# A decoder layer on one core: the sums for the up projection get a pool of their own, and the down projection's first tiles are staged in its room

## The chip, the cores and the metric

The kernel runs on one core of one Trainium2 chip. The core has a matrix engine (PE; its weight loads are listed apart as PEld), a vector engine (DVE), a scalar engine (ACT), GpSimd (POOL) and a sync engine (SP), which run side by side and wait for each other on semaphores. Transfers between DRAM and the on-chip memory (SBUF) are issued from an engine's queue (here almost all from SP's, some from POOL's) and land some microseconds later. The metric is the device time in microseconds (us); less is better. Before the change it is 2153.9 us, the median of three runs (2151.9 to 2154.32).

## The reference

One layer with 512 tokens of width 2048: token mixing, then a gated feed-forward block of width 5632 with a short causal convolution on one branch.

```
def conv_ffn(h, w_ffn_in, conv_w, conv_b, w_ffn_out):
    S = h.shape[1]
    up = h @ w_ffn_in
    a, b = up[..., :D_FF], up[..., D_FF:]
    a_pad = jnp.pad(a, ((0, 0), (CONV_W - 1, 0), (0, 0)))
    a = (conv_w[0] * a_pad[:, 0:S] + conv_w[1] * a_pad[:, 1:S + 1]
         + conv_w[2] * a_pad[:, 2:S + 2] + conv_b)
    return (jax.nn.gelu(a, approximate=True) * b) @ w_ffn_out
...
        h = rmsnorm(x, attn_pre_norm[l])
        m = token_mixer(h, w_in[l], ...)
        x = x + rmsnorm(m, attn_post_norm[l])
        h = rmsnorm(x, ffn_pre_norm[l])
        f = conv_ffn(h, w_ffn_in[l], conv_w[l], conv_b[l], w_ffn_out[l])
        x = x + rmsnorm(f, ffn_post_norm[l])
```

## The kernel before

**Numbers in two parts.** Every float32 operand of a large product is split into a high and a low part: ACT writes the high part (`whi` of a weight, L120; `ah` of an activation, L133), DVE the low part, operand minus high part (`wlo`, L121; `al`, L134). A product is then three matmuls: high by high, low by high, high by low. A "granule" is one weight tile of 128 x 1024 numbers (512 KB): its load, its `whi`, its `wlo`, and the matmuls that read them.

**Seven products for eight.** The up products (`h @ w_ffn_in`) and the down products (`@ w_ffn_out`) go by Winograd's form of Strassen's scheme: 2 x 2 blocks of activations and of weights, seven products of sums of blocks. A `Unit` runs seven segments, x0, z0, y0, z1, x1, y1, y2, which read the activation operands a11, s5, s2, s3, a12, s7, a22 in that order (s5, s2, s3, s7 are sums and differences of the a's), each with two granules. The weight sums are made on the way: POOL issues a DMA that adds a second weight block to a tile in place (`more`, L856), and DVE adds others (L872 in y0, L890 after y1). There are 20 up units (ten groups of 512 columns, two branches), then 10 down units (five chunks `c` of two groups, two halves `cb` of the output's columns). An up segment has 48 matmuls of 256 columns, a down segment 24 of 512. At the end `last_group` does the first 512 columns of the feed-forward width without the scheme, adds the shared part `accp` to the accumulators `acc` (L1128), and `finish` writes the output.

**From up to down.** After the last branch of a group, `token_sums` writes the group's blocks (a11, a12, a22) and, with DVE adds into tiles `s` (L975), its sums s5, s2, s7, s3 to DRAM (`sd0a`, `sd0s` for chunk 0, ... `sd4a`, `sd4s` for chunk 4). A tile `s` is one of two with tag "sum". `prepare(c, n)` (L993 to L996) loads operand n of chunk c from DRAM, 512 KB, and splits it into its place in `ah` and `al`. For chunk 0 it loads a11, s5, s2, s3 into free activation tiles (`flat_tile()`, rows named `u`), a12, s7, a22 later into staging tiles (`st`).

**Room in SBUF.** The up operands s5, s2, s3 (three sums in two parts, 6 tiles of 8 KB per partition), the tiles `s` and the p1 tiles lie in the pool `fa` up to the close:

```
    fa.close()
    sp3 = ctx.enter_context(tc.tile_pool(name="sp3", bufs=2, reuse_waits="tile"))
    ff = ctx.enter_context(tc.tile_pool(name="ff", bufs=2, reuse_waits="tile"))
    acc = [ff.tile([P, D], F32, name=f"acc{t}", bufs=1) for t in range(NT)]
```

`ff` holds the staging tiles (four with tag "st"), `acc`, `accp` and the gains `g3`; `sp3` holds spare granule tiles. They take `fa`'s room, so whoever writes there first waits for the last reader of what lay there.

**What sets the order.** The up and down units are ordered by a scheduler over the written program; each engine and SP's queue then run their own list in order. `to_ffn` (the norm ahead of the feed-forward block) and the last part of `last_group` are in hand-written order. In `to_ffn` the third token tile's `residual` (L647), `square` (L652) and `scale` (L658) stand among the loads and splits of weights (`weights_f`, L120 and L121) for matmuls at L156 to L158.

## Time and profile before

| | |
|---|---|
| device time, median of 3 runs | 2153.9 us (2151.9 to 2154.32) |
| profiled execution, its own time | 2150.73 us |
| its span | 2149.0 us |
| mean granted clock of PE | 0.995 |
| PE busy | 2110.2 us, 98% of the span |
| PEld busy | 1878.9 us, 87% |
| DVE busy | 1415.0 us, 66% |
| ACT busy | 899.1 us, 42% |
| POOL busy | 206.7 us, 10% |

The table is of one profiled execution; its span runs from its first to its last instruction. A row of the timeline has the start and the length in us, the engine, the line, the operation with output and input tiles, and in brackets how long the engine idled before it and what ended that. A row of the windows has a stretch, its length, the busy time and count of instructions of PE, PEld, DVE, ACT and POOL, then the granted clock of PE (1.00 is full), the DMA engines' share and GB/s. SPq and POOLq are the queues in which these engines issue transfers.

### The profile page before, as it was taken

To read this page: it belongs to the slowest core of one execution; us is meant where nothing else is said; L and a number is where in the kernel's file an instruction comes from. 1 tells how busy PE (TensorE), PEld (TensorE's weight loads), DVE (VectorE), ACT (ScalarE), POOL (GpSimd) and SP (SyncE) were. 2 spreads that over 40 slices of the span, in tenths; PEclk is the share of its full clock that TensorE was granted. 3 is DMA by queue.
4 is the path that set the end of the run, shared out by engine and by line. 5 is a ranking of instruction groups with operands and counts; after the bars stand their busy time and mean duration, and the time that the engine had idled before them with its cause. 6 is when DMAs were issued, how large, how long until landed. Compare 5 with 4: busy or idle time off the path is not lost.

```text
span 2149.0 us, 31874 instructions
## 1 busy us (share of the span) xinstructions
PE 2110.2 (98%) x13009; PEld 1878.9 (87%) x13009; DVE 1415.0 (66%) x1721; ACT 899.1 (42%) x1162; POOL 206.7 (10%) x245
## 2 busy tenths in 40 slices
PE   7999999999999999999999999999999899999997
PEld 6878888788888888999999999999999778888886
DVE  5345554443444237588777786787878777988987
ACT  4233332333343224344544553554454354544443
POOL 1000000000000000010111101111111011111101
PEclk9999999999999999999999999999999999999999
DMA  6322222222224234456775767667577677676663
GB/s 214 101 74 79 79 70 79 79 79 87 80 79 170 95 128 174 130 117 144 167 182 137 170 156 181 158 143 188 141 172 181 188 204 204 183 196 176 165 168 137
DMA packets 218470, 303.82 MB, mean 141 GB/s; under 512 B 11776, under 2 KB 155572, under 8 KB 216404
## 3 DMA queue, kind: packets, MB, share of 16 engines
q1 hardware_dynamic: 165204, 238.87, 33.0%
q0 software_dynamic: 53120, 62.92, 18.9%
q8 instruction: 102, 1.67, 0.3%
q14 instruction: 44, 0.36, 0.1%
HBM read 273.97 MB, written 27.79 MB: 140 GB/s over the span
## 4 chain that ended last, share of the span: by engine, by line
PE 39%; issue 16%; DVE 3%; DMA 2%; POOL 1%; ACT 1%; POOLq 0%; DVEq 0%; ACTq 0%
PE bank L908 7%; PE bank L909 7%; PE bank L907 7%; PE bank L1004 5%; PE bank L1005 4%; PE bank L1006 4%; PE bank L158 1%; PE bank L156 1%; PE bank L157 1%; DMA raw<-in_w_ffn_in_dram 1%; DVE wlo L121 1%; POOL rt L856 1%; DMA rt<-in_w_ffn_out_dram 1%; POOL raw L856 1%; DVE acc L1144 0%
## 5 line engine op out<-in xcount | busy, mean ns | idle before, releaser
L121 DVE TENSOR_TENSOR wlo<-raw,whi 128x1024 fp32r<-128x1024 f32 x332 | 404.1, 1221 | 371.5 <-ACT whi L120 354.5
L120 ACT ACTIVATE whi<-raw 128x1024 fp32r<-128x1024 f32 x332 | 350.9, 1060 | 647.5 <-PE bank L175 159.4
L120 ACT ACTIVATE whi<-rt 128x1024 fp32r<-128x1024 f32 x240 | 252.9, 1059 | 261.0 <-PE bank L908 157.4
L909 PE MATMUL bank<-ah,wlo 128*128 128x256 f32 x1280 | 353.6, 276 | 0.2 <-DVE wlo L121 0.2
L908 PE MATMUL bank<-al,whi 128*128 128x256 f32 x1280 | 353.4, 276 | 0.0
L907 PE MATMUL bank<-ah,whi 128*128 128x256 f32 x1280 | 353.3, 276 | 0.0
L121 DVE TENSOR_TENSOR wlo<-rt,whi 128x1024 fp32r<-128x1024 f32 x240 | 292.6, 1221 | 88.3 <-ACT whi L120 88.2
L174 PE MATMUL bank<-whi,ah 128*128 128x512 f32 x640 | 253.0, 398 | 0.4 <-ACT ah L133 0.4
L175 PE MATMUL bank<-wlo,ah 128*128 128x512 f32 x640 | 251.6, 394 | 0.1
L176 PE MATMUL bank<-whi,al 128*128 128x512 f32 x640 | 250.8, 394 | 0.0
L909 PEld LDWEIGHTS bank<-ah,wlo 128*128 128x128 f32 x1280 | 240.3, 188 | 0.4 <-DVE wlo L121 0.4
L908 PEld LDWEIGHTS bank<-al,whi 128*128 128x128 f32 x1280 | 240.3, 188 | 0.1
L907 PEld LDWEIGHTS bank<-ah,whi 128*128 128x128 f32 x1280 | 240.3, 188 | 0.1
L1005 PE MATMUL bank<-wlo,ah 128*128 128x512 f32 x560 | 219.9, 393 | 4.1 <-DVE wlo L121 4.1
L1004 PE MATMUL bank<-whi,ah 128*128 128x512 f32 x560 | 215.1, 393 | 6.6 <-ACT whi L120 4.7
L1006 PE MATMUL bank<-whi,al 128*128 128x512 f32 x560 | 219.1, 391 | 0.0
L156 PE MATMUL bank<-ah,whi 128*128 128x512 f32 (+1 forms) x576 | 215.1, 373 | 1.9 <-ACT whi L120 1.9
L158 PE MATMUL bank<-ah,wlo 128*128 128x512 f32 (+1 forms) x576 | 212.9, 370 | 0.8 <-DVE wlo L121 0.8
L157 PE MATMUL bank<-al,whi 128*128 128x512 f32 (+1 forms) x576 | 213.3, 370 | 0.0
L176 PEld LDWEIGHTS bank<-whi,al 128*128 128x128 f32 x640 | 120.8, 189 | 26.0 <-DVE al L134 0.3
L175 PEld LDWEIGHTS bank<-wlo,ah 128*128 128x128 f32 x640 | 121.0, 189 | 25.8 <-DVE wlo L121 1.0
L174 PEld LDWEIGHTS bank<-whi,ah 128*128 128x128 f32 x640 | 120.8, 189 | 24.9 <-ACT ah L133 0.8
(222 smaller groups left out, 3685.5 us busy)
## 6 DMA issues: line engine op xcount, KB each, us to landing
raw<-in_w_in_dram SPq DMA_DIRECT2D x96, 512.0 KB, 3.7
raw<-in_w_ffn_in_dram SPq DMA_DIRECT2D x96, 512.0 KB, 5.0
raw<-in_w_ffn_out_dram SPq DMA_DIRECT2D x48, 512.0 KB, 6.3
rt<-in_w_ffn_in_dram SPq DMA_DIRECT2D x40, 512.0 KB, 6.4
rt<-in_w_ffn_in_dram POOLq DMA_DIRECT2D x40, 512.0 KB, 5.9
raw<-in_w_ffn_in_dram POOLq DMA_DIRECT2D x40, 512.0 KB, 6.7
raw<-in_w_o_dram SPq DMA_DIRECT2D x32, 512.0 KB, 3.5
rt<-in_w_ffn_out_dram SPq DMA_DIRECT2D x20, 512.0 KB, 6.3
```

The lines of the kernel that those rows point to most:

```text
L120: act(hi, raw, AF.Copy)
L121: tt(lo, raw, hi.bitcast(F32), ALU.subtract)
L156: mm(o, wh, ah[:, t0:t1, kk, :], start=st, stop=False)
L174: mm(banks[t], ah[:, t, s, :], w[0][:, k, :], start=st, stop=False)
L175: mm(banks[t], ah[:, t, s, :], w[1][:, k, :], start=False, stop=False)
L176: mm(banks[t], al[:, t, s, :], w[0][:, k, :], start=False, stop=sp)
L907: mm(o, wh, sh[:, :, kk, :], start=start and kk == 0 and n == 0, stop=False, **NOW)
L908: mm(o, wh, sl[:, :, kk, :], start=False, stop=False, **NOW)
L909: mm(o, wl, sh[:, :, kk, :], start=False, stop=kk == HK - 1, **NOW)
L1004: mm(b[j], sh[:, o:o + P], w[0][:, q, :], start=start and st == 0, stop=False, **NOW)
L1005: mm(b[j], sh[:, o:o + P], w[1][:, q, :], start=False, stop=False, **NOW)
L1006: mm(b[j], sl[:, o:o + P], w[0][:, q, :], start=False, stop=st == 3, **NOW)
```

## The change

Six things are changed.

- The tiles of s5, s2, s3 of the up units move from pool `fa` to a pool `so`, which is closed after the last up unit's z1, the last segment that reads one of them (s3). Pool `ff` is opened there, in that room, with the four staging tiles, the spare granule tiles, `accp` and half of `acc`. Pool `fa` stays open to the end. The other half of `acc` and `g3` become activation tiles (`flat_tile()`), `acc` and `g3` go by halves of 1024 columns, and the small sums `ssf` go to another pool.
- `prepare` is parted: `stage(c, n)` loads into a staging tile, and `prepare` splits it. For chunk 0, a11, s5, s2, s3 are staged right after that z1, and a12, s7, a22 each as a staging tile comes free. The load of the first down unit's b22 weights has a name of its own (`fetch`) and is called ahead of the last up segment.
- In the last group's `token_sums`, s7 and s3 take the tag "p1" in place of "sum", so that its four sums have four tiles.
- The load of `g3` moves behind the first down unit, in two halves.
- In `to_ffn`, the weights' load and split `weights_f(wa, 0, 3, sp2)` stands ahead of `residual(3)`, where it stood behind `square(3)`.
- In `last_group` the adds of `accp` go by 512 columns (twelve of 128 x 512 for six of 128 x 1024), and the scratch tile of `gain` comes from `fa`. The padding behind `ident` is 32 numbers shorter.

```diff
--- before.py
+++ after.py
...
@@ -695,10 +695,10 @@
         ba = [bank(psm) for _ in range(2)]
         bb = [bank(psm) for _ in range(2)]
         mm_t(ba, 0, wa[0], 0, 2)
+        weights_f(wa, 0, 3, sp2)
         residual(3)
         turn(2, 0, 1, 2, 3)
         square(3)
-        weights_f(wa, 0, 3, sp2)
         mm_t(ba, 1, wa[1], 0, 2)
         mm_t(ba, 2, wa[2], 0, 2)
         scale(3)
@@ -734,8 +734,9 @@
 
     NG = NF // 4
     rp = ctx.enter_context(tc.tile_pool(name="rp", bufs=4, reuse_waits="tile"))
-    fa = ExitStack()
-    fp = fa.enter_context(tc.tile_pool(name="fa", bufs=2, reuse_waits="tile"))
+    fp = ctx.enter_context(tc.tile_pool(name="fa", bufs=2, reuse_waits="tile"))
+    sums = ExitStack()
+    so = sums.enter_context(tc.tile_pool(name="so", bufs=1, reuse_waits="tile"))
 
     ud0 = dram.tile([P, 4, S], F32, name="ud0")
     SN = ("a11", "a12", "a22", "s5", "s2", "s7", "s3")
@@ -786,7 +787,7 @@
     for n, (i, j) in part.items():
         up[n] = tuple(v[:, 2 * i:2 * i + 2, HK * j:HK * (j + 1), :] for v in (ah, al))
     for n in ("s5", "s2", "s3"):
-        up[n] = tuple(fp.tile([P, 2, HK, P], F32R, name=f"{n}{v}", bufs=1) for v in "hl")
+        up[n] = tuple(so.tile([P, 2, HK, P], F32R, name=f"{n}{v}", bufs=1) for v in "hl")
     s7raw = []
 
     def up_sums():
@@ -839,7 +840,7 @@
         def __init__(self, a, block, prods, chain, out):
             self.narrow = prods is up_prods
             self.a, self.block, self.prods, self.chain, self.out = a, block, prods, chain, out
-            self.banks = {}
+            self.banks, self.b22 = {}, None
 
         def run(self, seg, op, raws):
             c = seg[0]
@@ -866,8 +867,12 @@
             self.run("z0", "s5", self.t)
             self.out("z0", self.banks["z"])
 
+        def fetch(self):
+            self.b22 = [load(self.block(1, 1, g), self.a) for g in range(2)]
+
         def y0(self):
-            self.b22 = [load(self.block(1, 1, g), self.a) for g in range(2)]
+            if self.b22 is None:
+                self.fetch()
             for g in range(2):
                 tt(self.t[g], self.t[g], self.b22[g], ALU.add)
             self.run("y0", "s2", self.t)
@@ -971,7 +976,7 @@
             dma(sd[c][n][:, i, :].rearrange("p (n t) -> p n t", n=2), src)
 
         def add(n, x, y, op):
-            t = fp.tile([P, 2, 256], F32, name=n, tag="sum", bufs=2)
+            t = fp.tile([P, 2, 256], F32, name=n, tag="p1" if gi == NG - 1 and n in ("s7", "s3") else "sum", bufs=2)
             tt(t, x, y, op)
             put(n, t)
             return t
@@ -990,10 +995,16 @@
     def piece(v, t, h):
         return v[:, t, HK * h:HK * (h + 1), :].rearrange("p k c -> p (k c)")
 
-    def prepare(c, n, stage=None):
-        raw = stage or ff.tile([P, GR], F32, name="st", tag="st", bufs=4)
+    staged = {}
+
+    def stage(c, n):
+        raw = staged[c, n] = ff.tile([P, GR], F32, name="st", tag="st", bufs=4)
         dma(raw, sd[c][n].rearrange("p g x -> p (g x)"))
-        split(piece(ah, *place[n]), piece(al, *place[n]), raw)
+
+    def prepare(c, n):
+        if (c, n) not in staged:
+            stage(c, n)
+        split(piece(ah, *place[n]), piece(al, *place[n]), staged.pop((c, n)))
 
     def down_prods(b, op, g, w, start):
         sh, sl = (piece(v, *place[op]) for v in (ah, al))
@@ -1027,8 +1038,7 @@
                     continue
                 half, col, sign = {"z0": (1, 1, 1), "y0": (0, 1, -1), "z1": (0, 1, 1), "x1": (0, 0, 1),
                                    "y1": (1, 1, -1), "y2": (1, 0, 1)}[seg]
-                sl = slice(1024 * cb + 512 * col, 1024 * cb + 512 * (col + 1))
-                into(acc[2 * half + j][:, sl], b[j], sign, c == 0 and seg in ("z0", "y0", "x1", "y2"))
+                into(quarter(acc[2 * half + j], 2 * cb + col), b[j], sign, c == 0 and seg in ("z0", "y0", "x1", "y2"))
 
         return Unit(2, block, down_prods, chain, out)
 
@@ -1040,14 +1050,21 @@
             u.z0()
         u.y0()
         u.z1()
+        if nxt is None:
+            sums.close()
+            ff = ctx.enter_context(tc.tile_pool(name="ff", bufs=2, reuse_waits="tile"))
+            for n in ("a11", "s5", "s2", "s3"):
+                stage(0, n)
         if i == 0:
             for h, r in enumerate(s7raw):
                 split(up["s7"][0][:, h], up["s7"][1][:, h], r)
         if nxt is None:
-            prepare(0, "a11", flat_tile())
+            prepare(0, "a11")
+            stage(0, "a12")
         u.x1()
         if nxt is None:
-            prepare(0, "s5", flat_tile())
+            prepare(0, "s5")
+            stage(0, "s7")
         u.y1()
         if nxt is not None:
             nxt.x0()
@@ -1055,22 +1072,32 @@
             nxt.z0()
         else:
             downs = [down_unit(c, cb) for c in range(NG // 2) for cb in range(2)]
-            prepare(0, "s2", flat_tile())
+            prepare(0, "s2")
+            stage(0, "a22")
             downs[0].x0()
-            prepare(0, "s3", flat_tile())
+            prepare(0, "s3")
+            downs[0].fetch()
             u.y2()
-    fa.close()
-    sp3 = ctx.enter_context(tc.tile_pool(name="sp3", bufs=2, reuse_waits="tile"))
-    ff = ctx.enter_context(tc.tile_pool(name="ff", bufs=2, reuse_waits="tile"))
-    acc = [ff.tile([P, D], F32, name=f"acc{t}", bufs=1) for t in range(NT)]
     accp = [ff.tile([P, D // 2], F32, name=f"accp{j}", bufs=1) for j in range(2)]
-    g3 = ff.tile([P, D], F32, name="g3", bufs=1)
-    ssf = [ff.tile([P, 4], F32, name=f"ssf{t}", bufs=1) for t in range(NT)]
-    bcast_row(g3, ffn_post_norm[0])
+    acc = [None, None] + [[ff.tile([P, D // 2], F32, name=f"acc{t}", tag=f"acc{t}{b}", bufs=1) for b in range(2)]
+                          for t in (2, 3)]
+    for t in range(2):
+        acc[t] = [flat_tile() for _ in range(2)]
+    g3 = [flat_tile() for _ in range(2)]
+    ssf = [small.tile([P, 4], F32, name=f"ssf{t}", tag=f"ssf{t}", bufs=1) for t in range(NT)]
+
+    def quarter(v, c):
+        return v[c // 2][:, 512 * (c % 2):512 * (c % 2 + 1)]
+
+    sp3 = ff
+    small_pools.append(ff)
     downs[0].z0()
     for i, u in enumerate(downs):
         nxt = downs[i + 1] if i + 1 < len(downs) else None
         nc_ = (i + 1) // 2
+        if i == 1:
+            for b in range(2):
+                bcast_row(g3[b], ffn_post_norm[0, 1024 * b:1024 * (b + 1)])
         first = i % 2 == 0
         last_cb = i % 2 == 1 and nxt is not None
 
@@ -1112,20 +1139,21 @@
             mm(b, uh[:, tk], hi[:, k % 2, :], start=k == 0, stop=False)
             mm(b, uh[:, tk], lo[:, k % 2, :], start=False, stop=False)
             mm(b, ul[:, tk], hi[:, k % 2, :], start=False, stop=k == 3)
-        sl = slice(512 * c, 512 * (c + 1))
-        tt(acc[t][:, sl], acc[t][:, sl], b, ALU.add)
+        a = quarter(acc[t], c)
+        tt(a, a, b, ALU.add)
 
     def gain(t, c, eng):
-        sl = slice(512 * c, 512 * (c + 1))
-        jk = ff.tile([P, S], F32, name="jk6", tag="jk", bufs=1)
-        act(jk, acc[t][:, sl], AF.Square, accum_out=ssf[t][:, c:c + 1])
...
-                dst = acc[2 * half + j].rearrange("p (b c x) -> p b c x", b=2, c=2)[:, :, c, :]
-                tt(dst, dst, accp[j].rearrange("p (b x) -> p b x", b=2), op)
+                for b in range(2):
+                    dst = quarter(acc[2 * half + j], 2 * b + c)
+                    tt(dst, dst, accp[j][:, 512 * b:512 * (b + 1)], op)
         for c in range(2):
             gr = ffn_out_weights(gi, c)
             for t in range(NT):
...
```

**On ACT, at the turn from the up to the down units.** Before (rows of one engine in program order: line, operation, output and input tiles, shape; `ah<-u` is the split of an operand loaded into an activation tile, `ah<-st` into a staging tile, `whi<-rt` and `whi<-raw` are weight splits, `accp` is the first write of the shared part from a PSUM bank):

```order
L120 ACTIVATE whi<-rt 128x1024
L133 ACTIVATE ah<-u 128x1024
L120 ACTIVATE whi<-rt 128x1024
L133 ACTIVATE ah<-u 128x1024
L120 ACTIVATE whi<-rt 128x1024 x2
L1010 ACTIVATE accp_15929<-bank 128x512
L1010 ACTIVATE accp_15930<-bank 128x512
L120 ACTIVATE whi<-rt 128x1024 x2
L133 ACTIVATE ah<-st 128x1024
L120 ACTIVATE whi<-raw 128x1024
L1010 ACTIVATE acc_15927<-bank 128x512
L133 ACTIVATE ah<-st 128x1024
```

Now, with the changed kernel's line numbers (L1021 for L1010, L943 for L938):

```order
L120 ACTIVATE whi<-raw 128x1024 x5
L133 ACTIVATE ah<-st 128x1024
L120 ACTIVATE whi<-rt 128x1024
L133 ACTIVATE ah<-st 128x1024
L943 ACTIVATE u<-bank 128x2x256
L133 ACTIVATE ah<-st 128x1024
L120 ACTIVATE whi<-rt 128x1024
L133 ACTIVATE ah<-st 128x1024
L120 ACTIVATE whi<-rt 128x1024
L133 ACTIVATE ah<-st 128x1024
L120 ACTIVATE whi<-rt 128x1024
L1021 ACTIVATE accp_15935<-bank 128x512
```

Of the seven splits of chunk 0, four stood ahead of the first writes of `accp` and three behind them; now five stand ahead of the first write, the first of them just behind the last weights of the up units, one between the two writes and one right behind them.

**On DVE, at the same place.** Before (`al` is the low part of an operand, `s` a tile of `token_sums`; L940, L946 and L960 finish the last up unit):

```order
L946 TENSOR_TENSOR u<-bank,p_15483 128x2x256
L121 TENSOR_TENSOR wlo<-rt,whi 128x1024
L960 TENSOR_TENSOR u<-u 128x1024
L890 TENSOR_TENSOR rt<-rt,raw 128x1024
L975 TENSOR_TENSOR s_15906<-u 128x512
L975 TENSOR_TENSOR s_15909<-s_15906,u 128x512
L975 TENSOR_TENSOR s_15912<-u 128x512
L975 TENSOR_TENSOR s_15915<-s_15909,u 128x512
L121 TENSOR_TENSOR wlo<-rt,whi 128x1024
L872 TENSOR_TENSOR rt<-rt,raw 128x1024
L121 TENSOR_TENSOR wlo<-rt,whi 128x1024
L134 TENSOR_TENSOR al<-st,ah 128x1024
```

Now (L877 for L872, L945 for L940, L951 for L946, L965 for L960):

```order
L134 TENSOR_TENSOR al<-st,ah 128x1024
L121 TENSOR_TENSOR wlo<-rt,whi 128x1024
L134 TENSOR_TENSOR al<-st,ah 128x1024 x2
L121 TENSOR_TENSOR wlo<-rt,whi 128x1024
L945 TENSOR_TENSOR u<-u,bank 128x2x256
L134 TENSOR_TENSOR al<-st,ah 128x1024
L121 TENSOR_TENSOR wlo<-rt,whi 128x1024
L965 TENSOR_TENSOR u<-u 128x1024
L134 TENSOR_TENSOR al<-st,ah 128x1024
L121 TENSOR_TENSOR wlo<-rt,whi 128x1024
L134 TENSOR_TENSOR al<-st,ah 128x1024
L121 TENSOR_TENSOR wlo<-rt,whi 128x1024 x2
```

The four rows L975 stood in one piece ahead of a `wlo` of the first down unit's y0. Now they stand some ten rows further down, parted by weight splits, and all seven `al` stand ahead of them.

**On SP's queue.** Before (`u<-sd0a` and `u<-sd0s` load chunk 0's first operands, `raw` and `rt` are weights, `sd4s<-s` stores the last group's sums):

```order
L48 DMA rt<-in_w_ffn_out_dram 128x2x512 x2
L48 DMA u<-sd0a_6661 128x1024
L48 DMA raw<-in_w_ffn_out_dram 128x2x512 x4
L48 DMA u<-sd0s_6664 128x1024
L48 DMA u<-sd0s_6665 128x1024
L48 DMA u<-sd0s_6667 128x1024
...
L48 DMA sd4s_6694<-s_15912 128x512
L48 DMA sd4s_6695<-s_15915 128x512
L48 DMA g_15931<-in_ffn_post_norm_dram 128x2048
L48 DMA st<-sd0a_6662 128x1024
L48 DMA st<-sd0s_6666 128x1024
L48 DMA st<-sd0a_6663 128x1024
```

Now:

```order
L48 DMA rt<-in_w_ffn_out_dram 128x2x512 x2
L48 DMA raw<-in_w_ffn_out_dram 128x2x512 x2
L48 DMA st<-sd0a_6664 128x1024
L48 DMA st<-sd0s_6667 128x1024
L48 DMA st<-sd0s_6668 128x1024
L48 DMA st<-sd0s_6670 128x1024
L48 DMA raw<-in_w_ffn_out_dram 128x2x512 x2
L48 DMA st<-sd0a_6665 128x1024
L48 DMA st<-sd0s_6669 128x1024
L48 DMA st<-sd0a_6666 128x1024
L48 DMA st<-sd1a_6671 128x1024
L48 DMA rt<-in_w_ffn_out_dram 128x2x512
```

The load of a11 stood ahead of four weight loads, and the three loads of a12, s7, a22 behind the last group's stores; now all seven stand together, ahead of those stores, and a11's stands behind two of the weight loads.

More of the change, by code (lines that the diff above doesn't have):

```diff
@@ L63, in hybrid_layer @@
     wpool = ctx.enter_context(tc.tile_pool(name="w", bufs=6))
-    ident = const.tile([P, P + 104], F32, name="ident")[:, :P]
+    ident = const.tile([P, P + 72], F32, name="ident")[:, :P]
     make_identity(nc, ident)
@@ L1114, in ffn_out_part @@
             mm(b, ul[:, tk], hi[:, k % 2, :], start=False, stop=k == 3)
-        sl = slice(512 * c, 512 * (c + 1))
-        tt(acc[t][:, sl], acc[t][:, sl], b, ALU.add)
+        a = quarter(acc[t], c)
+        tt(a, a, b, ALU.add)
     def gain(t, c, eng):
-        sl = slice(512 * c, 512 * (c + 1))
-        jk = ff.tile([P, S], F32, name="jk6", tag="jk", bufs=1)
-        act(jk, acc[t][:, sl], AF.Square, accum_out=ssf[t][:, c:c + 1])
-        eng.tensor_tensor(acc[t][:, sl], acc[t][:, sl], g3[:, sl], ALU.mult)
+        a = quarter(acc[t], c)
+        jk = fp.tile([P, S], F32, name="jk6", tag="p1", bufs=2)
+        act(jk, a, AF.Square, accum_out=ssf[t][:, c:c + 1])
+        eng.tensor_tensor(a, a, quarter(g3, c), ALU.mult)
     def last_group(gi, us):
@@ L1143, in finish @@
                 sl = slice(512 * i, 512 * (i + 1))
-                stt(acc[t][:, sl], acc[t][:, sl], rs[t], x1[t][:, sl], ALU.mult, ALU.add)
+                a = quarter(acc[t], i)
+                stt(a, a, rs[t], x1[t][:, sl], ALU.mult, ALU.add)
                 if t == 3:
-                    dma(out2[t * P:(t + 1) * P, sl], acc[t][:, sl])
+                    dma(out2[t * P:(t + 1) * P, sl], a)
                 elif i % 2:
                     sl = slice(512 * i - 512, 512 * (i + 1))
-                    dma(out2[t * P:(t + 1) * P, sl], acc[t][:, sl])
+                    dma(out2[t * P:(t + 1) * P, sl], acc[t][i // 2])
         with tc.manual_schedule(engines=IN_ORDER):
```

## The prediction

> **What bounds the kernel now.** I read the shares of the page first, then whom PE waits for, then PE by windows around those waits, then PE, DVE, ACT and SP by timeline there.
>
> ```profile
> PE 2110.2 (98%) x13009; PEld 1878.9 (87%) x13009; DVE 1415.0 (66%) x1721; ACT 899.1 (42%) x1162; POOL 206.7 (10%) x245
> PE bank L1004 <- ACT whi L120: 4.7, 1, 4.7
> PE bank L1005 <- DVE wlo L121: 4.1, 4, 1.6
> PE bank L156 <- ACT whi L120: 1.9, 1, 1.9
> PE bank L1004 <- ACT acc L1010: 1.3, 1, 1.3
> PE bank L158 <- DVE wlo L121: 0.8, 1, 0.8
> 840.00:860.00 20.00, 17.30 (x132) 16.77 (x131) 15.66 (x18) 9.82 (x15) 0.92 (x3) 0.91 0.46 159
> 1600.00:1700.00 100.00, 100.00 (x859) 98.99 (x858) 74.22 (x74) 48.59 (x53) 12.68 (x10) 1.00 0.77 195
> 1700.00:1740.00 40.00, 29.93 (x108) 22.53 (x108) 26.16 (x27) 16.54 (x21) 2.38 (x2) 0.87 0.68 221
> 1740.00:1760.00 20.00, 20.00 (x90) 16.54 (x89) 15.00 (x14) 12.14 (x16) 2.38 (x2) 1.00 0.66 167
> ```
>
> PE is busy in 98% of the span, so an edit off PE gains only where PE stands still or runs slow. Two places that the change touches do so: L1004 and L1005, the first down unit, and L156 and L158, in `to_ffn`. From 1600 to 1700 us PE never stops. From 1700 to 1740 it is idle for 10.07 of 40 us and its clock is granted at 0.87. A down unit in full stride shows 90 matmuls in 20 us, 0.222 us each. The 108 of the gap would take 24.0 us, so **16.0 us are lost there**; by idle time and clock, 10.07 + 0.13 x 40 = 15.3. I take the middle, **15.7**.
>
> ```profile
> 1688.90 0.40 PE L1004 MATMUL bank<-whi,ah 128*128 128x512 f32 x1
> 1699.94 0.50 PE L1004 MATMUL bank<-whi,ah 128*128 128x512 f32 x1
> 1701.39 0.50 PE L1005 MATMUL bank<-wlo,ah 128*128 128x512 f32 x1 [0.95 <-DVE wlo L121]
> 1712.33 1.22 PE L1004 MATMUL bank<-whi,ah 128*128 128x512 f32 x2 [4.68 <-ACT whi L120]
> 1717.41 0.63 PE L1006 MATMUL bank<-whi,al 128*128 128x512 f32 x1
> 1717.84 0.63 PE L1004 MATMUL bank<-whi,ah 128*128 128x512 f32 x1
> 1725.15 0.64 PE L1005 MATMUL bank<-wlo,ah 128*128 128x512 f32 x1 [1.60 <-DVE wlo L121]
> ```
>
> The first down x0 starts at 1688.90, the last up segment y2 follows, and z0 starts at 1699.94: 11.04 us for two segments, 5.5 each. Behind the long waits matmuls start 0.43 us apart (1717.41, 1717.84), about half speed. What held the 4.68 us stands on the other engines:
>
> ```profile
> 1710.01 0.69 DVE L975 TENSOR_TENSOR s<-u 128x512 f32<-128x512 f32 x1 [1.38 <-DMA sd4s<-s]
> 1712.81 0.69 DVE L975 TENSOR_TENSOR s<-s,u 128x512 f32<-128x512 f32 x1 [2.10 <-DMA sd4s<-s]
> 1710.74 0.60 ACT L1010 ACTIVATE accp<-bank 128x512 f32<-128x512 f32 x1 [6.47 <-DVE s L975]
> 1720.51 1.06 ACT L133 ACTIVATE ah<-st 128x1024 fp32r<-128x1024 f32 x1 [3.44 <-DMA st<-sd0a]
> 1656.80 0.46 SPq L48 DMA_DIRECT2D u<-sd0a  x1
> 1676.20 7.34 SPq L48 DMA_DIRECT2D raw<-in_w_ffn_out_dram  x4
> 1714.37 0.46 SPq L48 DMA_DIRECT2D st<-sd0a  x1
> ```
>
> ACT writes `accp` into room that the tiles `s` leave, so it waits 6.47 us for DVE's L975; the `whi` that PE needs stands behind it. DVE itself waits there 1.38 and 2.10 us for the stores of the first two `s` tiles. And SP sends the loads of a12, s7, a22 only behind those stores, at 1714.37, whence the late split at 1720.51 and PE's waits at 1723 and 1725.
>
> **The change part by part.**
>
> *Removed at the turn.* `accp` now lies in the closed pool's room, whose last readers are matmuls of z1, long done: the 6.47 us on ACT go. L975 has four tiles: its 3.48 us of waits go, and it stands behind the splits. The three staging loads move ahead of the stores: the 3.44 us go. All causes of the 15.7 us are met; what is late next decides what comes back.
>
> *Late next: the splits of a11, s5, s2, s3.* Before, a11 was loaded at 1656.80 and split early. Now its load follows the end of z1.
>
> ```profile
> 1678.45 0.69 DVE L935 TENSOR_TENSOR u<-u,bank 128x512 f32<-128x512 f32 x1 [0.74 <-PE bank L909]
> 1723.88 1.22 DVE L121 TENSOR_TENSOR wlo<-raw,whi 128x1024 fp32r<-128x1024 f32 x1
> 1725.01 1.22 DVE L134 TENSOR_TENSOR al<-st,ah 128x1024 fp32r<-128x1024 f32 x1
> st<-sd0a SPq DMA_DIRECT2D x2, 512.0 KB, 6.1
> u<-sd0a SPq DMA_DIRECT2D x1, 512.0 KB, 6.6
> rt<-in_w_ffn_out_dram POOLq DMA_DIRECT2D x2, 512.0 KB, 7.6
> ```
>
> L935 waits for z1's last matmul and starts at 1678.45, so the load goes out at about 1678.3, between the second and third of SP's four `raw` loads. It lands 6.1 us later, 1684.4; ACT's `ah` takes 1.06; from 1685.45 DVE has it. A full split on DVE starts 1.13 us after the one before (1723.88, 1725.01). From a11's `al` to the `wlo` of z0's second granule DVE's order shows 13 such rows and one short one of 0.6: 15.3 us, so it ends at 1700.8. PE needs it 2.7 us (half a segment) after 1699.94: met, as is the granule before, at 1699.6. Behind stand two L877, the short L951, the `al` of a22 and the `wlo` of y0's first granule: 4 x 1.13 + 0.6 = 5.1, ending at 1705.9. PE wants that one matmul into y0, at 1699.94 + 5.5 + 0.2 = 1705.6. So **0.3 us** comes back; later granules have 2.7 us per 1.13 to 2.3 us of DVE, and the margin grows. DVE is thus full for 20 us, and each us that a11 lands later costs PE a us. Landings in the rows go to 7.6 us: 1.5 more. ACT's write of `accp` stands ahead of a `whi`, which cost 1.3 once before (the wait on L1010): up to 1.3 more. If such stalls fall together, the half clock returns: about 1.7 us, half of the 3.4 us that it lasts in `to_ffn` (below). So the return is 0 to 4.8; I take **2.0**, nearer the low end, since its first link is the 6.1 of the same kind of load.
>
> *Weighed: how long a load takes.* The row above has 6.1 us for such a load. "DMA: Bandwidth & Descriptors" of the Trainium skill (section "Anatomy of one DMA — SWDGE (gpsimd) path") gives about 2.0 us plus bytes over 436 GB/s, as an estimate 3.2 us for 512 KB issued by POOL; the POOL row above has 7.6, so the measurement decides. By the Trainium skill's figure nothing would come back and the gain at the turn would be 15.7.
>
> *Added on DVE, ACT, SP.* The splits are the same seven, moved; the shape of the L975 adds stays. `g3`'s load moves behind the first down unit; its reader is at the end, 350 us later. `accp`'s last adds go from 6 x 1.22 to 12 x 0.69 us, 1.0 us more on DVE among the last down units; DVE waits 2.71 us there for PE, so I take 0, at most 1.0.
>
> ```profile
> 2094.00 0.69 DVE L1012 TENSOR_TENSOR acc<-acc,bank 128x512 f32<-128x512 f32 x1 [2.71 <-PE bank L1006]
> 2095.78 1.22 DVE L1128 TENSOR_TENSOR acc<-acc,accp 128x1024 f32<-128x1024 f32 x1
> ```
>
> *`to_ffn`.*
>
> ```profile
> 846.63 0.38 PE L156 MATMUL bank<-ah,whi 128*128 128x256 f32 x1 [1.94 <-ACT whi L120]
> 847.89 0.39 PE L158 MATMUL bank<-ah,wlo 128*128 128x256 f32 x1 [0.76 <-DVE wlo L121]
> 848.29 0.42 PE L157 MATMUL bank<-al,whi 128*128 128x256 f32 x1
> 848.51 0.42 PE L158 MATMUL bank<-ah,wlo 128*128 128x256 f32 x1
> 851.64 0.28 PE L158 MATMUL bank<-ah,wlo 128*128 128x256 f32 x1
> 846.61 1.23 DVE L121 TENSOR_TENSOR wlo<-raw,whi 128x1024 fp32r<-128x1024 f32 x1 [0.67 <-ACT whi L120]
> 853.41 2.48 DVE L134 TENSOR_TENSOR al<-bank,ah 128x512 fp32r<-128x512 f32 x4 [1.79 <-ACT ah L133]
> ```
>
> PE waits 1.94 + 0.76 us for a split that stands behind `residual` and `square`, then starts matmuls 0.22 us apart until 851.64, 3.4 us at half speed. The split now stands ahead of both. But DVE has the same work in this stretch (15.66 of 20 us) and PE waits for DVE's next splits behind it; DVE can only shed its two idle times, 0.67 + 1.79 = 2.5. So 0 to 2.5; I take the middle, **1.3**.
>
> *Weighed: when the clock falls.* These rows show half speed after 2.7 us of idle time within 3.4 us. "TensorE: Matmul & The Clock Gate" of the Trainium skill (section "HAM oscillation — how this bites in real kernels") puts the rule as no idle gap over about 3.4 us. The trace disagrees: the gaps were 1.94 and 0.76. By the Trainium skill's rule a return of stalls under 3.4 us would never cost clock, and the upper end of the return would be 3.1 in place of 4.8.
>
> *Sum.* 15.7 - 2.0 + 1.3 = 15.0 us. The profiled execution would go from 2150.73 to 2135.7. The median of the runs, 2153.9, lies 3.2 above it; beside that median the forecast is **2138.9 us**, -0.7%.
>
> **The rivals.**
>
> *DVE is the next bound.* DVE is full from 1685 to 1706 with margins under 1 us, so a landing late by 3 us (the far row, 7.6, and waiting behind the two `raw` loads just ahead) or a POOL transfer in its way gives stalls of 5 to 10 us with the half clock: gain 6 to 11, 2143 to 2148. For it: the margins above, and SP's four `raw` in 7.34 us, which compete for the same DMA engines. Against: DVE did the same number of splits before with gaps.
>
> *Nothing comes back.* Loads of the same size show 3.5 us on the profile's page where little else moves (`raw<-in_w_o_dram`):
>
> ```profile
> raw<-in_w_o_dram SPq DMA_DIRECT2D x32, 512.0 KB, 3.5
> ```
>
> At that a11 lands 2.6 us earlier, no stall is left, and with the upper end at `to_ffn` the gain is 15.7 + 2.5 = 18.2: 2135.7 and a little below. Against: DMA is 0.68 to 0.77 busy here.
>
> *The change doesn't do what it says.* If the wait only changes place (the staging loads held by another tile in that room up to 1700 and more), PE waits in x0 instead of z0 for about as long: 2149 to 2157. Against: the last reader of that room is z1, over by 1678.45.
>
> *Slower.* a11 is the one operand that the change loads later, by 1678.3 - 1656.80 = 21.5 us, and x0 needs it at 1688.90. Each us past that is lost. Slower by over 0.2% needs 17.0 + 4.3 = 21.3 us lost in the place of the return, a11 split only by 1710, landed by 1708, 30 us after its issue; the rows show 7.6.
>
> **How the numbers follow.** About 0.2% (4.3 us) is what a measurement of this kernel can tell from no change. My forecast (2135.7 to 2143) has 0.55; nothing comes back (2131 to 2135.7) 0.13; DVE as the next bound (2143 to 2149.6) 0.21; the change doesn't do it (2149.6 to 2158.2) 0.08; slower 0.03. So faster 0.89, same 0.08, slower 0.03. The range runs from 2133 to 2147: it leaves out some 0.05 below and 0.14 above.
>
> **What would show it.** After the change the waits of PE should have no L1010-to-L975 chain: `whi` within 1 us of its tile, no row of 4.68. The window behind z0's start should show a clock of 0.95 or more and at most 2 to 3 us of idle time. a11's split should start by 1686 in before's time, and any stall should be PE's L1010 or L1011 rows waiting for `wlo` at y0. In `to_ffn` the two waits at L156 and L158 should be gone and the next split's wait stand in their place. I am wrong if a11's split starts after 1689, or if PE idles at x0, or if the half clock shows in the first down unit though its waits are short.

## Result and profile after

The changed kernel takes **2141.63 us** (median of 4 runs, 2137.54 to 2143.08) against 2152.9 us before (4 runs, 2150.48 to 2154.32): a ratio of 0.9946 with a 95% interval of 0.9928 to 0.9963. The interval leaves out 1, so it is faster, by 0.5%. The forecast was 2138.9 with a range of 2133 to 2147. The profiled execution went from 2150.73 to 2141.76 us, its span from 2149.0 to 2140.0.

The page of the changed kernel, its first line and its busy times, then whom PE waits for from 1600 us on (us in total, times, longest) and the windows at the turn (stretch, length, busy PE, PEld, DVE, ACT, POOL with counts, clock, DMA share, GB/s):

```profile
span 2140.0 us, 31884 instructions
PE 2106.5 (98%) x13009; PEld 1874.5 (88%) x13009; DVE 1415.4 (66%) x1727; ACT 899.9 (42%) x1162; POOL 206.3 (10%) x245
PE bank L1015 <- ACT acc L1021: 1.5, 1, 1.5
PE bank L1140 <- DVE wlo L121: 1.2, 2, 0.9
PE bank L1015 <- ACT whi L120: 1.2, 2, 0.6
PE bank L1015 <- DVE acc L1023: 1.1, 1, 1.1
PE bank L1016 <- DVE wlo L121: 0.9, 2, 0.5
1660.00:1700.00 40.00, 39.67 (x321) 38.28 (x320) 32.47 (x33) 23.45 (x26) 4.98 (x4) 1.00 0.74 211
1700.00:1740.00 40.00, 36.77 (x155) 28.53 (x155) 30.30 (x31) 18.94 (x22) 4.77 (x4) 1.00 0.90 266
```

The wait of 4.7 us is gone, the longest at the turn is 1.5, and the clock stays at 1.00. By the count used in the prediction, 155 matmuls at 0.222 us are 34.4 us, so 5.6 us are still lost between 1700 and 1740 where 16.0 were. DMA's share has risen from 0.68 to 0.90.

The rows behind this, from the changed kernel's timeline of PE, ACT, DVE and SP, its DMA issues between 1686 and 1694 us (tiles, queue, count, KB each, median us to landing), and then POOL's timeline, first of the changed kernel (L857), then of the kernel before (L856):

```profile
1703.63 0.73 PE L1015 MATMUL bank<-whi,ah 128*128 128x512 f32 x2 [0.61 <-ACT whi L120]
1704.89 0.50 PE L1016 MATMUL bank<-wlo,ah 128*128 128x512 f32 x1 [0.53 <-DVE wlo L121]
1709.74 0.50 PE L1015 MATMUL bank<-whi,ah 128*128 128x512 f32 x1 [1.48 <-ACT acc L1021]
2078.46 0.50 PE L1140 MATMUL bank<-wlo,ah 128*128 128x512 f32 x1 [0.85 <-DVE wlo L121]
1683.85 1.06 ACT L133 ACTIVATE ah<-st 128x1024 fp32r<-128x1024 f32 x1 [1.36 <-DMA st<-sd0a]
1698.08 1.06 ACT L120 ACTIVATE whi<-rt 128x1024 fp32r<-128x1024 f32 x1 [1.80 <-DMA rt<-in_w_ffn_out_dram]
1702.52 1.06 ACT L120 ACTIVATE whi<-rt 128x1024 fp32r<-128x1024 f32 x1 [2.90 <-DMA rt<-in_w_ffn_out_dram]
1684.94 1.23 DVE L134 TENSOR_TENSOR al<-st,ah 128x1024 fp32r<-128x1024 f32 x1 [1.20 <-ACT ah L133]
1677.20 0.44 SPq L48 DMA_DIRECT2D st<-sd0a  x1
rt<-in_w_ffn_out_dram POOLq DMA_DIRECT2D x2, 512.0 KB, 10.8
1687.61 1.19 POOL L857 DMA_DIRECT2D rt<-in_w_ffn_out_dram  x1 [13.24 <-DVE wlo L121]
1691.17 1.20 POOL L857 DMA_DIRECT2D rt<-in_w_ffn_out_dram  x1 [2.36 <-DVE wlo L121]
1686.17 1.19 POOL L856 DMA_DIRECT2D rt<-in_w_ffn_out_dram  x1 [10.81 <-DVE wlo L121]
1688.88 1.20 POOL L856 DMA_DIRECT2D rt<-in_w_ffn_out_dram  x1 [1.51 <-DVE wlo L121]
```

a11 is issued at 1677.20, split on ACT at 1683.85 and on DVE at 1684.94, as forecast to half a us (PE is 1.0 us ahead of before here). But ACT, whose `whi` for z0 is wanted next, waits 1.80 and 2.90 us for `rt`, the weight tile into which POOL's transfer adds. POOL issues two such transfers. One by one they take 10.4 and 11.3 us, where they took 7.4 and 7.7 before.

They also go out later. Each waits for a `wlo` on DVE, and these two `wlo` now stand behind the splits of a11, s5 and s2 in DVE's queue. Against PE's progress the two issues are 2.4 and 3.3 us later than before (1.4 and 2.3 by the clock, and PE is 1.0 us ahead). So `rt` lands 5.4 and 6.9 us later against PE, of which 3.0 and 3.6 are the longer transfer and the rest is the later issue.

**Where the time went, stage by stage.** PE issues the same number of matmuls in every kernel here, in the same order but for some rows around the turn and at the end of the down units. So the start of its n-th matmul in one trace can be set against that in another. The table has by how many us PE gains (+) or loses (-) against the profiled kernel before in each stage: `to_ffn` (820 to 860 us), the up units from there to the first down x0 (1688.90), the turn (to 1728.90), the down units (to 2087), and the first products of `last_group`. Each row is one execution.

| kernel | to_ffn | up | turn | down | last_group | time, us |
|---|---|---|---|---|---|---|
| changed | +1.95 | -1.28 | +10.74 | -1.73 | -1.15 | 2141.63 (4 runs) |
| changed, again | +1.97 | -0.87 | +11.26 | -6.37 | -1.29 | 2142.0 (5 runs) |
| to_ffn undone | +1.53 | -1.25 | +10.62 | -3.30 | -1.53 | 2144.37 (1 run) |
| before + tags | +0.05 | -0.79 | +4.69 | -4.47 | -0.04 | 2151.28 (1 run) |
| tags undone | +1.93 | +0.01 | +10.89 | -3.73 | -1.31 | 2142.18 (1 run) |
| chunk 1 late | +1.93 | -0.72 | +9.84 | -3.85 | -1.13 | 2140.38 (4 runs) |
| a12, s7, a22 late | +1.95 | -1.01 | +13.84 | -8.40 | -0.83 | 2146.95 (10 runs) |
| both late | +1.92 | -0.18 | +13.12 | -4.36 | -1.63 | 2140.3 (4 runs) |
| before + split adds | +0.07 | -0.57 | +1.28 | -2.23 | -1.49 | 2153.41 (1 run) |
| a11 early | +1.93 | -3.59 | +11.15 | -6.80 | -1.95 | 2144.76 (10 runs) |
| gains late | +1.93 | +0.73 | +11.11 | +1.23 | -1.95 | 2139.45 (5 runs) |
| all late | +1.95 | +0.51 | +13.11 | -4.30 | -1.47 | 2142.41 (5 runs) |

The times are medians of each kernel's own runs, beside which the kernel before took 2152.9 to 2154.4 us; the execution in a row is the slowest of its runs for "changed, again", "chunk 1 late", "both late" and "a11 early", the fastest for "gains late" and "all late", and the profiled one of the kernel before (2150.73 us) lies 2.2 us under its median.

How far the stages vary by themselves can be read from the two rows of the changed kernel and from "before + split adds", which is the kernel before up to the last adds: 1.3 us at the turn, several us in the down units. With a11 early, the wait ahead of x0 falls into the column of the up units.

### The profile page after: what moved, and what is told of

It reads as the page before. It is cut to its first block, busy times and chain, and to the rows that moved or that the text cites. A ratio compares the mean times of both kernels' runs of the same rounds, so it can differ in the third digit from the quotient of the medians.

```text
span 2140.0 us, 31884 instructions
## 1 busy us (share of the span) xinstructions
PE 2106.5 (98%) x13009; PEld 1874.5 (88%) x13009; DVE 1415.4 (66%) x1727; ACT 899.9 (42%) x1162; POOL 206.3 (10%) x245
## 4 chain that ended last, share of the span: by engine, by line
PE 30%; issue 22%; DVE 3%; DMA 2%; POOL 2%; ACT 0%; POOLq 0%; DVEq 0%; SPq 0%; ACTq 0%
PE bank L914 6%; PE bank L912 6%; PE bank L913 6%; PE bank L1016 3%; PE bank L1017 3%; PE bank L1015 3%; PE bank L158 1%; PE bank L156 1%; PE bank L157 1%; DMA rt<-in_w_ffn_out_dram 1%; DVE wlo L121 1%; POOL rt L857 1%; POOL raw L857 1%; DMA raw<-in_w_ffn_in_dram 1%; PE bank L1140 0%
## 5 line engine op out<-in xcount | busy, mean ns | idle before, releaser
L1015 PE MATMUL bank<-whi,ah 128*128 128x512 f32 x560 | 213.0, 390 | 3.8 <-ACT acc L1021 1.5
```

The costliest lines, as they stand in the source:

```text
L1015: mm(b[j], sh[:, o:o + P], w[0][:, q, :], start=start and st == 0, stop=False, **NOW)
```

## Experiments

**The edit in to_ffn undone** (changed kernel).

```diff
-        weights_f(wa, 0, 3, sp2)
         residual(3)
         turn(2, 0, 1, 2, 3)
         square(3)
+        weights_f(wa, 0, 3, sp2)
```

> The changed kernel with the weights' load and split in to_ffn put back behind square(3). My reading of the trace (PE 2.0 us earlier behind to_ffn, of which the prediction had 1.3): the two waits of PE at L156 and L158 of 1.9 and 0.8 us and the half clock come back, the span is about 2.0 us longer than the changed kernel's 2140.0, so near 2142, and the turn from up to down stays as in the changed kernel, so that it serves as a second look at the turn: POOL's accumulating transfers of rt there take 10 us or more again, and PE idles about 3.2 us between 1700 and 1740. Rival: PE's gain in to_ffn is given back by a later wait, then the span stays at 2140.

Its time was 2144.37 us in one run, its span 2142.7. PE's timeline in `to_ffn`:

```profile
846.44 0.39 PE L156 MATMUL bank<-ah,whi 128*128 128x256 f32 x1 [1.90 <-ACT whi L120]
847.70 0.39 PE L158 MATMUL bank<-ah,wlo 128*128 128x256 f32 x1 [0.76 <-DVE wlo L121]
847.92 0.28 PE L156 MATMUL bank<-ah,whi 128*128 128x256 f32 x1
848.04 0.28 PE L157 MATMUL bank<-al,whi 128*128 128x256 f32 x1
```

The two waits are back, but behind them matmuls start 0.12 us apart: no half clock this time. So of the 1.95 us that the changed kernel gained here, 0.42 is left for the edit in this execution (1.95 - 1.53); the rest is the half clock, which followed the same two waits in the kernel before and in both kernels built on it. Most of the longer span lies in the down units. The turn repeated itself, 10.6 us.

**The tags alone** (kernel before).

```diff
-            t = fp.tile([P, 2, 256], F32, name=n, tag="sum", bufs=2)
+            t = fp.tile([P, 2, 256], F32, name=n, tag="p1" if gi == NG - 1 and n in ("s7", "s3") else "sum", bufs=2)
```

> The kernel before with one edit: s7 and s3 of the last group take the tag p1, so that the four sums have four tiles. Theory: of the 15.7 us lost at the turn, the two waits of L975 for stores (1.38 and 2.10 us) stand in the chain of the 4.68 us wait of PE; they go, ACT's write of accp waits for DVE about 3 us in place of 6.47, and the staging loads go out some 3 us sooner, but still behind the stores: the span falls by 3 to 5 us, to 2144 to 2146, and a half clock stays. Rival: the room of the closed pool is what counts; accp waits for the last reader of the sums all the same, and the span falls by less than 1.5 us.

One run, 2151.28 us. PE's waits from 1600 us on, and ACT's timeline at `accp`:

```profile
PE bank L1005 <- DVE wlo L121: 4.8, 7, 1.6
PE bank L1004 <- ACT whi L120: 3.1, 1, 3.1
1710.12 0.60 ACT L1010 ACTIVATE accp<-bank 128x512 f32<-128x512 f32 x1 [4.89 <-DVE s L975]
```

The wait for the stores was one part of the 4.7 us: PE's wait falls to 3.1, ACT's from 6.47 to 4.89 (3 was expected), and the turn gains 4.7 us. In the rows ACT still waits for L975, so what is left is the room that `accp` takes over; no run changes that room alone. The span did not fall, since this execution lost 4.5 us in the down units; one run can't tell that from the spread.

**The tags undone** (changed kernel; the edit above the other way round).

> The changed kernel with s7 and s3 of the last group back on the tag of the two sum tiles. In the kernel before, that edit alone gave 4.5 us at the turn. Theory: with the splits staged early and accp in other room, nothing that PE needs soon stands behind the four sums any more (the scheduler puts the third and the fourth some rows further down), so the turn keeps its 10.7 us within 0.7 and the span is 2139 to 2142. Rival: DVE is so full at the turn that each wait for a store costs PE 1 to 3 us, span 2142 to 2145.

One run, 2142.18 us, turn 10.9. With the splits staged early and `accp` elsewhere, nothing that PE needs soon stands behind the four sums. The edit that gave 4.7 us at the turn by itself gives nothing beside the others. So the gain at the turn comes from the rest that acts there, the new room, the early staging loads and the later load of `g3`; no run parts the first two.

**Staging loads held back.** A copy of one column, which the load overwrites, ties a load to a later result. First three of chunk 1's loads alone:

```diff
         raw = staged[c, n] = ff.tile([P, GR], F32, name="st", tag="st", bufs=4)
+        if c == 1 and n in ("a11", "s5", "s2"):
+            act(raw[:, :1], accp[0][:, 512:513], AF.Copy)
         dma(raw, sd[c][n].rearrange("p g x -> p (g x)"))
```

> The changed kernel with the staging loads of chunk 1 (a11, s5, s2, s3; needed some 60 us later) held back by a copy of one column that depends on a result of the second down unit; the column is overwritten by the load. Theory A, the DMA engines are crowded by staging loads when POOL's accumulating transfers run: three of the seven or eight loads in the way are gone, the second accumulating transfer takes 9 to 10 us in place of 11.3, PE's waits between 1700 and 1712 (0.6, 0.5, 1.5) shrink, the time falls by 0.5 to 2 us to some 2139.5 to 2141. Theory B, what came back is DVE's and ACT's full queues: nothing changes at the turn (2141.6).

2140.38 us (4 runs, 2138.26 to 2145.61), turn 9.8: nothing that can be told from the changed kernel. POOL's two transfers still take 10.4 us (median), so these three loads are not what lengthens them. This execution's wait in y0 is 1.48 us as in the changed kernel, but 3.4 us of half clock follow it (matmuls 0.43 us apart from 1711.25 us on, a mean clock of 0.96 between 1700 and 1740), so the 9.8 has a loss in it that the changed kernel's profiles lack. Then a12, s7, a22 as well, staged behind `downs[0].z0()` and tied to the first write of `accp`:

```diff
+        if c == 0 and n in ("a12", "s7", "a22"):
+            act(raw[:, :1], accp[0][:, :1], AF.Copy)
```

> As the run with chunk 1 held back, and the loads of a12, s7, a22 of chunk 0 also held back, until the first write of accp. Theory A, crowded DMA engines: only the two weight loads stand in the way; POOL's accumulating transfers take 7.5 to 8.5 us as in the kernel before, ACT's whi of z0 no longer waits 1.8 and 2.9 us for them, the three waits of PE between 1700 and 1712 go, and the time falls by 2.5 to 4 us, to 2137.5 to 2139. Theory B, full DVE and ACT queues: the splits of a12, s7, a22 come in a less full stretch too, so PE's wait at y2 (0.33) and y0 shrink by 1 us at most, but the accumulating transfers still take over 10 us, and the time is 2140.5 to 2142.

2140.3 us (4 runs, 2139.42 to 2141.92). Its window at the turn, its DMA issues between 1686 and 1694 us, and ACT's timeline some us later:

```profile
1700.00:1740.00 40.00, 37.92 (x163) 30.36 (x164) 31.53 (x32) 20.13 (x28) 4.77 (x4) 1.00 0.85 237
rt<-in_w_ffn_out_dram POOLq DMA_DIRECT2D x2, 512.0 KB, 6.1
1721.14 1.06 ACT L120 ACTIVATE whi<-raw 128x1024 fp32r<-128x1024 f32 x1 [7.37 <-DMA raw<-in_w_ffn_out_dram]
```

POOL's transfers take 6.1 us in place of 10.8, and the turn gains 13.1 us, close to the 13.7 forecast. That settles one half of what the forecast had missed: **the loads of a12, s7 and a22 crowd the DMA engines while POOL's transfers run**. Against PE, POOL issues as late here as in the changed kernel (2.4 and 3.5 us later than before), so what changed is the length of the transfers. A rival is that DVE's work slows them, since the splits of those three operands are also gone from this stretch. But DVE is busy for 5.9 of the 6.3 us of the first transfer here, and for 4.1 of the 7.4 us in the kernel before. The DMA engines are full during it in all three kernels (share 0.96 or more) and move some 1.3 MB here, 2.0 before and 3.3 in the changed kernel (211, 265 and 321 GB/s over its length). But the time is that of the changed kernel within its spread. The loads only move: ACT waits 7.37 us for `raw` a little later, and 1.8 us are lost up to 1760 and 2.0 more up to 1800. With a12, s7, a22 held back and chunk 1 left free:

> The changed kernel with only the loads of a12, s7, a22 held back until the first write of accp, and chunk 1's as the pools let them. Theory A, DMA engines crowded while POOL's accumulating transfers run: those transfers take 6 to 8 us in place of 10 to 11, the turn gains 12.5 to 13.5 us against the kernel before in place of 10.7; what the run with both held back then lost up to the third down unit (3.9 us) is smaller, since chunk 1's loads are not moved into that unit: time 2137.5 to 2140. Rival: that loss comes from the splits of a12, s7, a22 on DVE and from the weights behind those loads, not from chunk 1; then it comes back here too, and the time is 2140 to 2142 again.

2146.95 us (10 runs, 2144.25 to 2150.26), a ratio to before of 0.9972 (0.9961 to 0.9983): slower than the changed kernel. POOL's first two transfers take 6.1 us here too, with chunk 1's loads free, so a12, s7 and a22 are the loads that count for them. ACT's and PE's timelines:

```profile
1723.65 1.06 ACT L120 ACTIVATE whi<-raw 128x1024 fp32r<-128x1024 f32 x1 [9.62 <-DMA raw<-in_w_ffn_out_dram]
1724.76 1.22 PE L1017 MATMUL bank<-whi,ah 128*128 128x512 f32 x2 [4.89 <-ACT whi L120]
```

The turn gains 13.8 us and 8.4 go back behind it: now chunk 1's loads and those of `g3` meet the next weights, PE waits 4.89 us, and the half clock comes behind that wait (matmuls 0.43 us apart for some 5 us). My theory of the transfers held, my forecast of the time (2137.5 to 2140) did not.

**The adds of accp by 512 columns alone** (kernel before).

```diff
-                dst = acc[2 * half + j].rearrange("p (b c x) -> p b c x", b=2, c=2)[:, :, c, :]
-                tt(dst, dst, accp[j].rearrange("p (b x) -> p b x", b=2), op)
+                for b in range(2):
+                    dst = acc[2 * half + j][:, 1024 * b + 512 * c:1024 * b + 512 * (c + 1)]
+                    tt(dst, dst, accp[j][:, 512 * b:512 * (b + 1)], op)
```

> The kernel before with one edit: the adds of accp in last_group by 512 columns, twelve of 128x512 for six of 128x1024. The changed kernel lost 1.2 us against before at the first products of last_group (PE waits 0.85 us for a wlo at the first weight granule). Theory: the smaller adds do this, by 1.0 us more on DVE and by another order there: PE waits 0.7 to 1.3 us more at that place than in the kernel before, span about 2150. Rival: PE comes there earlier relative to its loads, whatever the adds: then PE waits there as little as before (under 0.3 us).

One run, 2153.41 us. PE's waits from 1600 us on, of which before had 0.3 here:

```profile
PE bank L1113 <- DVE wlo L121: 1.5, 2, 1.2
```

The smaller adds are the cause: 1.5 us lost at this place, as in every kernel that has them (0.8 to 2.0), and none in the one kernel that leaves them as before (0.04, with the tags alone).

**a11 loaded early** (changed kernel; `stage` also takes a tile to load into).

```diff
...
+        if nxt is None:
+            stage(0, "a11", flat_tile())
         u.z1()
...
-            for n in ("a11", "s5", "s2", "s3"):
+            for n in ("s5", "s2", "s3"):
```

> The changed kernel with a11 of chunk 0 loaded early into a free activation tile, as the kernel before did, the rest staged as in the changed kernel. The prediction had the late a11 as the head of a chain in which each us costs PE a us. Theory DVE-full: with a11's split at 1671 the chain starts at s5, DVE gains a step of 1.13 us, PE's waits at y2 (0.2 and 0.3 us) go and those in z0 and y0 shrink by about 1 us: turn 11.5 to 12.5 us, time 2139.5 to 2141. Theory A, crowded DMA engines: only the two short waits at y2 go; POOL's transfers still take 10 us or more, z0 and y0 wait as long as in the changed kernel, time within 1 us of 2141.

2144.76 us (10 runs, 2143.22 to 2151.02), a ratio to before of 0.9959 (0.9947 to 0.9972). That is no faster than the changed kernel (0.9946, 0.9928 to 0.9963), but the intervals overlap, so that it is slower isn't shown. ACT's and PE's timelines at x0, in an execution of 2151.02 us, 6.3 above the median:

```profile
1688.73 1.06 ACT L133 ACTIVATE ah<-st 128x1024 fp32r<-128x1024 f32 x1 [6.83 <-DMA st<-sd0s]
1690.79 0.50 PE L1015 MATMUL bank<-whi,ah 128*128 128x512 f32 x1 [2.02 <-ACT whi L120]
1692.24 0.79 PE L1016 MATMUL bank<-wlo,ah 128*128 128x512 f32 x1 [0.95 <-DVE wlo L121]
```

Neither theory had this. With a11 out of the way the scheduler put the split of s5 ahead of x0's first `whi` on ACT. s5's load came late, ACT stood 6.83 us in its queue, and PE waited with it, with half clock behind. The order on ACT is that of every run, but the half clock is not: the mean clock is 0.996 in this execution and 0.998 in the other nine. How long they waited for s5 isn't known, so this explains the 2151.02 us and only perhaps the median. In the changed kernel a11's split is first, and x0's `whi` stands behind it and ahead of s5's.

**The changed kernel again, and the gains' loads late.** `g3`'s loads in the eighth down unit, tied to `accp` likewise:

```diff
-        if i == 1:
+        if i == 7:
             for b in range(2):
+                act(g3[b][:, :1], accp[0][:, :1], AF.Copy)
                 bcast_row(g3[b], ffn_post_norm[0, 1024 * b:1024 * (b + 1)])
```

> The changed kernel once more, unchanged, beside the next two runs on one chip. Theory (what the down units lose behind the turn, 2.9 us in the first profile against 1.2 in the kernel before, are short waits at fixed places whose size differs from execution to execution): the turn again gains 10 to 11.5 us against the kernel before, PE waits at the same places in the down units with other sizes, and 1.1 to 1.6 us more than before go at the first products of last_group; time 2140 to 2143. Rival: the loss in the down units is the same in size and place, then it belongs to the change.

> The changed kernel with the two loads of g3 (1 MB) held back to the eighth down unit by a copy of one column that the load overwrites; in the changed kernel they go out at 1711.6, among the last staging loads and ahead of POOL's transfers of the next weights. Theory A, the DMA engines are the scarce thing at the turn: PE's wait of 0.56 at 1721.5 goes, the two transfers of POOL at 1713 to 1717 land sooner, turn 11.2 to 12 us, time 0.5 to 1.5 us below the changed kernel. Rival: the loads are in nobody's way, time and turn as in the changed kernel within 0.5 us.

On one chip the changed kernel took 2142.0 us (5 runs, 2141.1 to 2145.45), that with the gains late 2139.45 (5 runs, 2137.0 to 2141.3), with ratios to before of 0.9945 (0.9932 to 0.9959) and 0.9934 (0.9921 to 0.9947). The intervals overlap; four of its five runs lie below the lowest of the changed kernel's five. From PE's waits from 1600 us on in the changed kernel's second profile, then PE's timeline in it, then the other kernel's window at the turn:

```profile
PE bank L1015 <- DVE acc L1023: 3.2, 5, 1.2
1720.88 0.73 PE L1015 MATMUL bank<-whi,ah 128*128 128x512 f32 x2 [1.02 <-ACT whi L120]
```

```profile
1700.00:1740.00 40.00, 37.58 (x162) 29.72 (x161) 33.79 (x34) 23.07 (x28) 4.77 (x4) 1.00 0.79 225
```

The wait at 1721, 0.56 and 1.02 us in the two profiles of the changed kernel, is gone with the gains late, and DMA's share falls to 0.79. Up to 1760 us the changed kernel's two profiles lost 0.8 and 1.3 us behind the turn, this one nothing. So about 1 us at that place is `g3`'s loads; the turn itself gains no more (11.1), and the rest of the 2.5 us between the medians isn't settled. The profiled run with the gains late took 2137.0 us and lost nothing in the down units, while that of the changed kernel took 2145.45 and lost 6.4 us there, much of it in waits of L1015 for `acc` up to 1.2 us. Such waits differ from execution to execution of the same kernel: my theory that they come at fixed places held, but 6.4 us is more than I had thought of.

Last, all three groups of loads held back:

> Chunk 1's loads, those of a12, s7, a22 and those of g3 all held back (the run with both held back, and g3's loads in the eighth down unit). There PE gained 13.1 us at the turn and lost 3.9 us up to the third down unit, the first of it behind a wait of ACT of 7.4 us for raw, a weight tile into which POOL adds, while g3's 1 MB was loaded. Theory A: without g3's loads that wait shrinks by 2 us or more, PE's waits of 1.2 and 0.5 us at 1716.7 and 1722.3 go in part, and the time is 2137 to 2139.5, below the changed kernel on the same chip by 1 to 3 us. Rival: the order of the splits of a12, s7, a22 on DVE makes those waits; time as in the run with both held back, within 1 us of the changed kernel.

2142.41 us (5 runs, 2140.66 to 2144.76). The turn gains 13.1 us, ACT's wait for `raw` shrinks from 7.37 to 4.84, but its next one grows from 2.84 to 5.24, and 2.6 us still go behind the turn, up to 1800 us: not better than the changed kernel.

## Why the prediction was right, point by point

- **The mechanism at the turn: right.** The chain from the stores over L975 and `accp` to `whi` is gone, and with it the 4.7 us wait and the half clock. The staging loads go out when they were forecast to, and x0 doesn't wait for a11.
- **The gain at the turn: right in kind, too large in size.** 13.7 us were forecast (15.7 less a return of 2.0); 10.7 and 11.3 were measured. The term that was mis-sized is the return: 2.0, with an upper end of 4.8. It measured 4.4 to 5.0 by stages and 5.6 by the window. I had led it along DVE's queue from a11's landing, and that chain came out: y2's wait is 0.33 us and DVE's split of z0's first weights isn't late on its own account. What I hadn't priced is what the staged operands do to another transfer of the same time, POOL's adds into `rt`. Their splits on DVE hold up its issue by 2.4 and 3.3 us, and the loads of a12, s7 and a22 lengthen it, from 7.6 us in my rows to 10.8. So the late a11 did cost PE time, but over POOL's transfer and ACT's `whi` in z0; the sign I had named, PE waiting for `wlo` at y0 first, didn't come. PE's waits in z0 and y0 (0.61, 0.53, 1.48) stand behind it, and with those loads held back they shrink, from 2.6 us in all to between 1.1 and 1.6, and the turn gives 13.1 to 13.8. The rival "DVE is the next bound" named a POOL transfer in the way only in passing.
- **Half clock in the return: didn't come, in part by luck.** The clock is 1.00 at the turn in both profiles of the changed kernel. But the run with chunk 1 late has the same wait of 1.48 us in y0, and there 3.4 us of half clock follow it.
- **to_ffn: 1.3 forecast, 1.95 measured, with another make-up.** The reorder saves 0.4 us where the clock stays full and about 1.5 more where the same waits would have halved it. My working took the size from DVE's idle time and not from the clock, so that it came near is luck in part. The bound from DVE's idle time (2.5) held.
- **accp's last adds: 0 forecast, at most 1.0; 1.15 to 1.3 lost.** DVE's idle 2.71 us lies elsewhere than the queue in front of the first `wlo` of `last_group`. The adds stand ahead of that `wlo`, and PE waits for it.
- **The down units: not in the sum.** The two executions of the changed kernel lost 1.7 and 6.4 us there against the profiled kernel before. A kernel that is the one before up to there lost 2.2, so most of this is spread, and that the change adds to it is neither shown nor excluded.
- **The sum.** 15.0 us forecast against the profiled execution, 9.0 measured, 11.3 between the medians. The return (3.0) and the adds (1.2), less what to_ffn gave more (0.7), are 3.5 of the 6.0 us that are missing against the profiled execution; the rest is about what the up units (1.3) and the down units (1.7) lost, which the sum left out and which vary by as much between executions. The medians agree better (3.7 us missing) since the profiled execution of the kernel before was 2.2 us under its median; that is luck and no merit of the sum.

## What to carry to other kernels

A transfer that is moved into a full stretch is paid by the others in flight: list every transfer between its new place and the time that its data is needed, and ask which of them PE waits for next, and what its issue waits for in turn. Three ways to hold the same loads back gained 2 to 3 us at this turn, and lost 2.6 to 9.7 us up to 1800 us, where the changed kernel lost 0.8 and 1.3. And where an edit splits a step into smaller ones, look at what stands right behind it in that engine's queue, not at the engine's idle time nearby.

## What the runs showed of the hardware

- Two waits of PE of 1.9 and 0.76 us in the same place were followed by half clock in the kernel before and in two variants of it, and by none in the run with the edit in to_ffn undone. "TensorE: Matmul & The Clock Gate" of the Trainium skill (section "Part 1: The HAM clock gate (the "warmup" mystery)") calls the window in which activity is counted free-running; these four traces agree with that, in that the same waits do and don't halve the clock. So do six profiles with a wait of 1.47 to 1.49 us at one place in y0 (the changed kernel twice, to_ffn undone, tags undone, chunk 1 late, gains late): only chunk 1 late has half clock behind it.
- An adding transfer of 512 KB issued by POOL took 6.1 us to land at the turn with the loads of a12, s7 and a22 held back, 7.6 to 8.4 in the kernel before and the two built on it, and 10.3 and 10.8 in the two profiles of the changed kernel (medians of two transfers each). "DMA: Bandwidth & Descriptors" of the Trainium skill (section "Queues, rings and completion order") says that each DMA engine goes round the queues that have work, packet by packet; the slower landing beside more loads of another queue agrees with it, though no run here shows the order of the packets.
